# A tenth column unit by seven products, less filler in each attention cycle, and scalings that change engine

## The chip, the cores and the metric

The kernel runs on one core of one Trainium2 chip. The metric is the device time of one execution in microseconds (us), as the median of several runs. The core has five engines with queues of their own, and each queue runs in order: TensorE (PE, matrix products), VectorE (DVE), ScalarE (ACT), GpSimd (POOL) and SyncE (SP, which here only issues transfers). An engine that waits for something holds up everything that stands behind it in its queue.

## The reference

One encoder layer: RMS norm of x (2048 rows of 1024), one projection to q, k, v and a gate, neighbourhood attention with 16 heads of 64 over a grid of 32 rows by 64 columns, gating, an output projection with a residual, and a last RMS norm.

```python
h = rmsnorm(x, norm_0)
q, k, v, gate = split(h @ w_in_0, 4)                  # 2048 x 1024 each
for each grid row r, for each block of 16 query columns:
    s = q . k / 8 + bias    over 8 grid rows and 32 columns, -1e30 outside a window of 16 columns
    o = softmax(s) @ v
x = x + (o * silu(gate)) @ w_out_0
out = rmsnorm(x, norm_f)
```

All of it is in float32.

## The kernel before

Every float32 operand of a large product is split into a rounded high part and a low part, and a product is made of three TensorE instructions of 128x512 (high by high, high by low, low by high). Such an instruction is called a product here. The projection is cut into units: q, k and gate have four units each, named ("k", 3) and so on, and one unit gives two pairs of heads. Stage one works on the first 1024 rows, stage two on the last 1024. There `seven_products` computes a unit as a 2 by 2 block matrix in Strassen's way, with seven block products of 12 instructions, 84 in all, in place of the 96 of the plain way. Stage two does so with the units in `units_two`. What is left of the last 1024 rows (`halves`, computed by `group` in the plain way, 24 products for one output tile) is not computed there but kept as filler.

Then comes attention in 32 cycles, one for each pair of heads and quarter of the rows: eight cycles of row quarter 0, then sixteen that take quarters 1 and 2 in turn, then eight of quarter 3. Tiles of quarters 0 and 3 are smaller (11 and 12 key rows, against 15). Pass m of the loop at the end of the program issues, in this order:

- filler products through `feed`, `amount[m]` of them. After the first eight `normalise(2m-1)` is issued; it takes the reciprocal of the softmax sums and scales the four tiles of the second half of cycle m-1, two on GpSimd (L1168) and two on ScalarE (L1166)
- `turns(m-1)`: 44 transposes of the scaled tiles into six banks of PSUM, which ScalarE and VectorE copy to SBUF, three banks each (`pta`, L1183 and L1185)
- `scores(2m)` and `scores(2m+1)`: products of queries and keys (L1139); VectorE adds the bias and takes the maxima (L1148), ScalarE takes the exponential with the row sums (L1154). `normalise(2m)` is issued within and scales its four tiles on GpSimd
- `values(m-1)`: the products with v (L1213), and on VectorE the gating (`og`, L1217).

Below, "stretch m" is the time from the first transpose of pass m to that of pass m+1. In it the scores, the exponentials and the scalings of cycle m are made, and its filler is `amount[m+1]`, to within a few products. The filler's first part are the units left over; the rest are output rows: `outputs()` computes the tiles 0 to 5 (`PLAIN`) with `w_out` in the plain way, and VectorE adds the residual (`add_rows`, L1289), ScalarE squares (L1292). Weights are split for it on ScalarE and VectorE (`wh`/`wl`, `woh`/`wol`, L192 to L198), and so are the attention rows (`split_og`, `gh`/`gl`, L1259 and L1260). Of a finished tile `root` makes 1/sqrt with eight small VectorE instructions (L1316 to L1323), `scale` multiplies with two instructions of 128x512 (L1331), `send` stores.

Then `rows_by_seven` computes the ten last row tiles as five pairs by seven products, 35 blocks of 12 instructions, in the order of `seq`. A block (m, P) has its operand formed five blocks earlier (`form_rows`, L1465 and L1466). After P = 7 GpSimd issues a transfer that adds rows of x onto a tile kept in SBUF (`p`, L1480); after P = 4 VectorE adds that tile (L1289).

There is no scheduler: each engine's order is that in which the code issues. `store(key, lag, f)` delays f by `lag` filler products, and `due` runs what has come due.

```python
    dense, end_of_it = 16.5, 24
    amount = [dense] * 25
    for m in range(8, 24):
        amount[m] += 1.5 if m % 2 == 0 else -1.5
```

Of the kernel before, what the change touches and what calls it, by code (L numbers as in the profile page):

```python
# [76 lines left out]
def build(ctx, tc, x, xr, xt, wg, bias, w_out, n0, nf, out):  # L77
# [169 lines left out]
    def units(k, j):  # L247
        return [KINDS[k] + j + i for i in range(2 if k == "v" else 1)]

    units_two = [(k, j) for j in range(3) for k in "kqg"]  # L250
    halves = [(k, 3, 1, c) for g in ("k", "qg") for c in (2, 3) for k in g]
    attending = [False]
    last_use = {}
    for n, (k, j, ph, c) in enumerate(halves):
# [792 lines left out]
    def projections():  # L1047
        for n, (kind, j, ph, c) in enumerate(halves):
            state["half"] = n
            w = (KINDS[kind] + j, ph)  # L1050
            for a in range(2):
                if n == len(halves) - 5 and a == 0:
                    for k in range(RES_EARLY):
                        load_res(*turns_[k])
                if n == len(halves) - 1:
                    if a == 0:
                        load_og(0)
                        load_og(1)
                    else:
                        store(("og0",), 9, lambda: split_og(0))  # L1060
                consume(1)
                p = yield from group(w, a, c, n)
                state["event"] = clock[0]
                give(kind, 2 * j + a, c, p, True)
            state["done_halves"] = n + 1
# [91 lines left out]
    def normalise(i, both=False, between=None):  # L1157
        st = ST.pop(i)
        nc.vector.reciprocal(st[:, 8:12], st[:, 4:8])  # L1159
        for j, C in enumerate(pairs[i][2]):  # L1160
            if j and between:
                between()
            for s in range(2):
                o = 8 + 2 * j + s
                if both and j:
                    nc.scalar.activation(X[i, C][s], X[i, C][s], AF.Copy, scale=st[:, o:o + 1])  # L1166
                else:
                    nc.gpsimd.tensor_scalar(X[i, C][s], X[i, C][s], st[:, o:o + 1], 1.0, op0=OP.mult, op1=OP.mult)  # L1168

    spots = linear()  # L1170

# [170 lines left out]
        else:  # L1342
            roots.append((clock[0] + 8, n, root, scale, send))

    roots = []
    ended = [False]

    def run_roots(most=99):
        while roots and most and (roots[0][0] <= clock[0] or ended[0]):
            most -= 1  # L1350
            _, n, root, scale, send = roots.pop(0)
            root()
            store(("y", n), 18, scale)
            store(("y", n), 36, send)

    turns_ = [(0, 0), (1, 0), (2, 0), (0, 1), (1, 1), (2, 1)] + [(n, j) for n in range(3, PLAIN) for j in range(2)]
    place = {}
# [166 lines left out]
    def rows_by_seven():  # L1524
# [1 line left out]
            TF[f] = [(woh[4 * r + k, c], wol[4 * r + k, c]) for k in range(4)]  # L1526
        E, LEAD = 3, 5
        seq = [(m, P) for P in (1, 2) for m in range(E)]
        seq += [(0, 6), (1, 6), (0, 7), (0, 5), (1, 7), (0, 4), (1, 5), (0, 3), (1, 4), (2, 6), (1, 3), (3, 1), (2, 7), (2, 5), (2, 4), (2, 3)]
        seq += [(m, P) for m in range(E, len(PAIRS)) for P in order7 if (m, P) not in seq]  # L1530
        todo = {}

        def on(i, f, *a):
# [36 lines left out]
                        f(*a)  # L1570

    cycles = len(order)
    dense, end_of_it = 16.5, 24
    amount = [dense] * 25
    first = 16
    amount[0] -= first / 2
# [56 lines left out]
    for m in range(cycles + 1):  # L1633
        a = amount[m] - 8
        begin(m)
        feed(8)
        if m:
            due_here = []
            quiet[0] = True
            if a < 12 and m > 8 and m % 2:  # L1640
                normalise(2 * m - 1, True, lambda: due_here.append(split_rows() or consume(1, turn=True)))
            else:
                normalise(2 * m - 1, True)
            if a > 12:
                run_roots()
            elif not rows_due():
                run_roots(1)
            for k in range(3):
                if m == 1 and k == 2:
                    pass  # L1650
                elif a > 12 or not any(due_here) and (k < 1 or k < 2 and m > 8 and m % 2 == 0):
                    got = split_rows()
                    due_here.append(got)
                    if not got:
                        consume(1, turn=True)
                    elif a < 12 and m % 2 == 0 and len(items) - state["used"] == 8:
                        feed(a * 0.2)
                        consume(1, turn=True)
                feed(a * 0.2)
        else:  # L1660
            feed(a * 0.6)
        quiet[0] = False
        feed(a * 0.4, 8 if a > 12 else 4)
        if m:
            turns(m - 1)
        if m == cycles:
            all_loads()
            feed(6)
# [12 lines left out]
        if m:  # L1681
            values(m - 1)
        runs[0] += 1
        if m == 20:
            late_loads()
    ended[0] = quiet[0] = True
    store(("roots",), 8, run_roots)
    while next(outs, 0) != 0:
        due(1)
    rows_by_seven()  # L1690
# [32 lines left out]
```

## Time and profile before

| | |
|---|---|
| median of 3 runs | 1019.54 us (1019.34 to 1019.98) |
| the profiled execution | 1020.12 us, span 1018.4 us |
| TensorE clock granted | 0.999 |
| PE, busy share of the span | 99% |
| DVE, ACT, POOL | 73%, 53%, 16% |
| stage two by seven products | 400.86 to 572.23 us |
| attention, first transpose to last | 587.70 to 910.61 us |
| output rows by seven products | 914.95 to 1012.37 us |

Times in the rows are from the span's start. A row of the timeline gives the start, the time that an instruction or a run of like instructions took, the engine, the line, what it writes and reads, and in brackets how long the engine had been idle and what it waited for. Products are pipelined: one shows about 0.39 us but the next starts about 0.23 us later, so that PE can lose some tenths without looking idle; the distance of two starts is the surer measure.

### The profile page before, as it was taken

What the parts mean: (1) busy time and instruction counts of PE and PEld (TensorE: products, weight loads), DVE (VectorE), ACT (ScalarE), POOL (GpSimd) and SP (SyncE); (2) the same over time, 40 slices, a digit from 0 to 9 for tenths busy, and PEclk for the clock granted to TensorE, in tenths of its full rate; (3) what the DMA queues carried; (4) which work ended last, traced back from release to release, by engine and by line L of the source; (5) the groups of instructions that cost most, each with busy time, mean ns of one, the idle gap of its engine ahead of it and who ended that gap; (6) DMA issues with size and microseconds to landing.
All of it is one profiled execution on the core that took longest, in us unless ns stands there. A gap on an engine that the chain in (4) does not pass through costs nothing.

```text
span 1018.4 us, 19622 instructions
## 1 busy us (share of the span) xinstructions
PE 1007.5 (99%) x6952; PEld 803.5 (79%) x6952; DVE 744.4 (73%) x1648; ACT 537.2 (53%) x1305; POOL 165.8 (16%) x244
## 2 busy tenths in 40 slices
PE   9999999999999999999999999999999999999997
PEld 6888888888788888888888777777777777778876
DVE  5385878899798876766776566577777787677876
ACT  7655323434435442343433477678788867663433
POOL 0000132232132000000000023233232323221010
PEclk9999999999999999999999999999999999999999
DMA  9734676575537846657455787879888689799453
GB/s 307 251 104 115 188 214 220 173 228 185 166 104 217 255 126 185 201 175 225 168 197 191 224 261 242 261 224 289 268 260 267 205 257 298 208 358 362 134 156 104
DMA packets 142602, 218.23 MB, mean 214 GB/s; under 512 B 13032, under 2 KB 60392, under 8 KB 142504
## 3 DMA queue, kind: packets, MB, share of 16 engines
q1 hardware_dynamic: 140632, 213.96, 66.3%
q0 software_dynamic: 1440, 2.62, 1.6%
q8 instruction: 55, 0.90, 0.3%
q10 hardware_dynamic: 432, 0.40, 0.1%
q14 instruction: 43, 0.35, 0.1%
HBM read 151.92 MB, written 65.01 MB: 213 GB/s over the span
## 4 chain that ended last, share of the span: by engine, by line
PE 93%; DVE 3%; DMA 1%; ACT 1%; issue 1%; SPq 0%; ACTq 0%; DVEq 0%
PE pp L438 38%; PE py L1494 9%; PE pv L562 8%; PE o L1213 7%; PE pv L948 7%; PE s L1139 7%; PE ph L1194 4%; PE pp L384 2%; PE pp L386 2%; PE pp L382 2%; PE po L1412 2%; PE po L1414 2%; PE po L1416 2%; ACT x L1154 1%; DVE f L421 1%
## 5 line engine op out<-in xcount | busy, mean ns | idle before, releaser
L438 PE MATMUL pp<-h,f 128*128 128x512 f32 x672 | 217.3, 389 | 0.0
L1168 POOL TENSOR_SCALAR x<-x,st 128x360 f32<-128x360 f32 (+5 forms) x192 | 97.2, 523 | 482.8 <-DVE st L1159 480.9
L1154 ACT ACTIVATE x<-x,st 128x360 f32<-128x360 f32 (+5 forms) x256 | 134.1, 525 | 29.9 <-DVE st L1148 29.9
L438 PEld LDWEIGHTS pp<-h,f 128*128 128x128 f32 x672 | 126.1, 188 | 26.1
L438 PE MATMUL pp<-t,f 128*128 128x512 f32 x558 | 141.7, 389 | 0.1
L438 PE MATMUL pp<-l,f 128*128 128x512 f32 x336 | 130.7, 389 | 0.0
L438 PEld LDWEIGHTS pp<-t,f 128*128 128x128 f32 x558 | 104.6, 188 | 22.3 <-DVE u L451 0.6
L458 POOL TENSOR_TENSOR tmp<-tmp,rb 128x512 f32<-128x512 f32 x36 | 59.0, 1641 | 268.5 <-DVE tmp L456 233.4
L1148 DVE CUSTOM_DVE_ANT_0 x<-s,em 128x360 f32<-128x360 f32 (+5 forms) x256 | 101.5, 451 | 1.4 <-PE s L1139 1.4
L421 DVE TENSOR_TENSOR f<-raw,f 128x512 fp32r<-128x512 f32 x105 | 75.1, 715 | 29.3 <-ACT f L420 29.1
L1213 PEld LDWEIGHTS o<-pta,vt 120*64 120x64 f32 (+2 forms) x1024 | 68.7, 137 | 22.6 <-DVE st L1148 15.2
L1213 PE MATMUL o<-pta,vt 120*64 120x192 f32 (+5 forms) x1024 | 83.4, 316 | 0.3 <-issue 0.3
L420 ACT ACTIVATE f<-raw 128x512 fp32r<-128x512 f32 x105 | 63.6, 622 | 31.4 <-DMA raw<-in_wg_dram 13.3
L1139 PE MATMUL s<-kt,q 64*64 64x360 f32 (+5 forms) x1024 | 79.1, 421 | 0.6 <-DVE pta L1183 0.5
L1183 DVE COPY pta<-ph 120x512 f32<-120x512 f32 (+5 forms) x96 | 56.0, 637 | 30.9 <-PE ph L1194 30.5
L438 PEld LDWEIGHTS pp<-l,f 128*128 128x128 f32 x336 | 63.1, 188 | 13.2
L1185 ACT ACTIVATE pta<-ph 120x512 f32<-120x512 f32 (+5 forms) x96 | 46.7, 558 | 37.0 <-PE ph L1194 37.0
L1139 PEld LDWEIGHTS s<-kt,q 64*64 64x64 f32 x1024 | 39.6, 131 | 24.7 <-DVE pta L1183 6.1
L438 PE MATMUL pp<-sixths,f 128*128 128x512 f32 x198 | 54.6, 389 | 0.0
L420 ACT ACTIVATE f<-s 128x512 fp32r<-128x512 f32 x42 | 26.3, 625 | 52.9 <-DVE s L427 49.3
L1194 PEld LDWEIGHTS ph<-ident,x 64*120 64x120 f32 (+2 forms) x1408 | 42.6, 128 | 11.3 <-issue 10.6
L1494 PE MATMUL py<-woh,f 128*128 128x512 f32 x160 | 50.4, 390 | 0.0
(209 smaller groups left out, 1910.1 us busy)
## 6 DMA issues: line engine op xcount, KB each, us to landing
raw<-in_wg_dram SPq DMA_DIRECT2D x120, 256.0 KB, 4.9
row<-in_xr_dram SPq DMA_DIRECT2D x32, 256.0 KB, 5.3
vd<-v SPq DMA_DIRECT2D x32, 256.0 KB, 2.8
sgd<-sg SPq DMA_DIRECT2D x32, 256.0 KB, 3.6
q<-qd SPq DMA_DIRECT2D x32, 256.0 KB, 5.5
sgt<-sgd SPq DMA_DIRECT2D x32, 256.0 KB, 6.7
ogd<-og SPq DMA_DIRECT2D x32, 256.0 KB, 3.2
kt<-kd SPq DMA_DIRECT2D x16, 480.0 KB, 6.7
```

The costliest lines, as they stand in the source:

```text
L420: nc.scalar.activation(t[:, 0], src, AF.Copy)
L421: nc.vector.tensor_tensor(t[:, 1], src, t[:, 0].bitcast(F32), OP.subtract)
L438: nc.tensor.matmul(B[n, P], t[:, int(m == 2), c], x[k][int(m == 1)], start=P in (1, 6, 5) and k == 0 and m == 0, stop=k == 3 and m == 2, s ...
L562: nc.tensor.matmul(ps[t], a[:, o], b, start=k == 0 and m == 0, stop=k == NK - 1 and m == 2)
L948: nc.tensor.matmul(ps, a[:, o], b, start=P in (1, 6, 5) and k == 0 and m == 0, stop=k == 3 and m == 2, skip_group_check=True)
L1139: nc.tensor.matmul(pst[s][h * 64:h * 64 + 64], qt[a, g * 64:g * 64 + 64], kt[a, :r1 - r0, c0:c0 + 8 * WIDE[C]].rearrange("p r (s c) -> p s ...
L1148: nc.vector.tensor_tensor_reduce(X[i, C][s], pst[s], EM[p, ROW_TYPE[T]][C > 0][s], -1.0, 1e38, OP.add, OP.min, st[:, o:o + 1])
L1154: nc.scalar.activation(X[i, C][s], X[i, C][s], AF.Exp, bias=st[:, o:o + 1], scale=-1.0, accum_out=st[:, 4 + o:5 + o])
L1168: nc.gpsimd.tensor_scalar(X[i, C][s], X[i, C][s], st[:, o:o + 1], 1.0, op0=OP.mult, op1=OP.mult)
L1194: nc.tensor.transpose(ph[b, h][:k, o:o + 64], X[2 * m + late_, group[g]][s][q, at:at + k], ident[q, q])
L1213: nc.tensor.matmul(o[s * 64:s * 64 + 64, g0 * 64:g1 * 64], vt[:k, strip, s * 64:s * 64 + 64], t[:k, n * 64:(n + g1 - g0) * 64], start=stri ...
L1494: nc.tensor.matmul(B[m, P], t[:, a, c], b, start=P in (1, 6, 5) and k == 0 and i == 0, stop=k == 3 and i == 2, skip_group_check=True)
```

## The change

Five things are done.

1. The unit ("k", 3) moves from the filler to stage two. `units_two` has ten entries, `halves` four instead of six. 96 products leave the filler and 84 come to stage two, so that the program has 12 fewer.
2. `dense` goes from 16.5 to 13.6, and with the shorter sum what the last cycles get falls as well. Counted in the order of the code, the filler products of stretches 1 to 31 are, before: 18 15 16 17 16 17 18 15 18 15 21 12 21 15 17 15 18 15 18 15 18 15 16 17 16 17 19 14 16 18 20 (518), and after: 10 14 13 14 14 13 15 12 16 12 16 12 15 13 15 12 15 12 18 9 15 12 14 13 13 13 13 14 13 15 20 (425). The first loads of attention rows, of residual rows and of the last norm's weights (`late_loads`, after pass 8 instead of 20) move with it, and `split_og(0)` has a lag of 14.
3. In `normalise` the two scalings on ScalarE become VectorE `tensor_scalar` instructions, and the work that was issued between the two pairs of scalings (`between`: a split) is issued behind both.
4. `run_roots` issues the roots, and a new `run_scales` issues the scaling of the tiles whose root was made in an earlier pass, right behind the next `normalise`; before, `scale` came 18 products after the root, wherever that fell.
5. In `rows_by_seven` the last blocks of a pair, P = 3 and P = 4, come behind the first block of the next pair, in this order; before, each pair from the fourth on ran 1, 6, 2, 7, 5, 4, 3 (its first block in one case ahead of the pair before it).

```diff
-    units_two = [(k, j) for j in range(3) for k in "kqg"]
-    halves = [(k, 3, 1, c) for g in ("k", "qg") for c in (2, 3) for k in g]
+    units_two = [(k, j) for j in range(3) for k in "kqg"] + [("k", 3)]
+    halves = [(k, 3, 1, c) for c in (2, 3) for k in "qg"]
...
-                    if a == 0:
+                    if a == 1:
                         load_og(0)
                         load_og(1)
-                    else:
-                        store(("og0",), 9, lambda: split_og(0))
+                        store(("og0",), 14, lambda: split_og(0))
...
         for j, C in enumerate(pairs[i][2]):
-            if j and between:
-                between()
             for s in range(2):
                 o = 8 + 2 * j + s
                 if both and j:
-                    nc.scalar.activation(X[i, C][s], X[i, C][s], AF.Copy, scale=st[:, o:o + 1])
+                    nc.vector.tensor_scalar(X[i, C][s], X[i, C][s], st[:, o:o + 1], None, op0=OP.mult)
                 else:
                     nc.gpsimd.tensor_scalar(X[i, C][s], X[i, C][s], st[:, o:o + 1], 1.0, op0=OP.mult, op1=OP.mult)
+        if between:
+            between()
...
             root()
-            store(("y", n), 18, scale)
-            store(("y", n), 36, send)
+            rooted.append((n, scale, send))
+
+    def run_scales():
+        while rooted:
+            n, scale, send = rooted.pop(0)
+            scale()
+            store(("y", n), 18, send)
...
-        seq += [(0, 6), (1, 6), (0, 7), (0, 5), (1, 7), (0, 4), (1, 5), (0, 3), (1, 4), (2, 6), (1, 3), (3, 1), (2, 7), (2, 5), (2, 4), (2, 3)]
-        seq += [(m, P) for m in range(E, len(PAIRS)) for P in order7 if (m, P) not in seq]
+        seq += [(0, 6), (1, 6), (0, 7), (0, 5), (1, 7), (0, 4), (1, 5), (0, 3), (1, 4), (2, 6), (1, 3), (2, 7), (2, 5)]
+        for m in range(E, len(PAIRS)):
+            seq += [(m, 1), (m - 1, 3), (m - 1, 4), (m, 6), (m, 2), (m, 7), (m, 5)]
+        seq += [(len(PAIRS) - 1, 4), (len(PAIRS) - 1, 3)]
...
-    dense, end_of_it = 16.5, 24
+    dense, end_of_it = 13.6, 24
...
                 normalise(2 * m - 1, True)
+            run_scales()
             if a > 12:
                 run_roots()
...
-        if m == 20:
+        if m == 8:
             late_loads()
```

Line numbers of the changed program are a few lower or higher than those of the profile: L1182 is the copy of L1183, L1158 the reciprocal of L1159, L1330 the scaling of L1331, L1288 the addition of L1289.

The first place is stretch 10, on ScalarE, from the last exponential of the cycle to the copies of the next transposes. Before:

```order
L1154 ACTIVATE x_7047,st<-x_7047,st 128x360
L1154 ACTIVATE x_7048,st<-x_7048,st 128x360
L197 ACTIVATE woh<-raw 128x512
L1166 ACTIVATE x_7047<-x_7047,st 128x360
L1166 ACTIVATE x_7048<-x_7048,st 128x360
L197 ACTIVATE woh<-raw 128x512
L368 ACTIVATE q<-pp 128x512
```

The same place on ScalarE after the change:

```order
L1153 ACTIVATE x_7173,st<-x_7173,st 128x360
L1153 ACTIVATE x_7174,st<-x_7174,st 128x360
L1258 ACTIVATE gh<-ograw 128x512 x2
L1232 ACTIVATE acc_173<-acc_173 128x512
L1232 ACTIVATE acc_174<-acc_174 128x512
```

The two scalings are gone from ScalarE, and the split of the first attention rows (`gh`) stands where a weight's did. On VectorE the same stretch ran, from the gating to the copies of the next transposes, before:

```order
L1217 TENSOR_TENSOR og<-o,sgt 128x512
L1159 RECIPROCAL st<-st 128x4
L198 TENSOR_TENSOR wol<-raw,woh 128x512 x2
L1183 COPY pta<-ph_7124 120x8x64
L1183 COPY pta<-ph_7126 120x8x64
L1183 COPY pta<-ph_7128 120x6x64
```

And on VectorE after the change:

```order
L1216 TENSOR_TENSOR og<-o,sgt 128x512
L1259 TENSOR_TENSOR gl<-ograw,gh 128x512 x2
L1158 RECIPROCAL st<-st 128x4
L1163 TENSOR_SCALAR x_7173<-x_7173,st 128x360
L1163 TENSOR_SCALAR x_7174<-x_7174,st 128x360
L1182 COPY pta<-ph_7241 120x8x64
L1182 COPY pta<-ph_7243 120x8x64
L1182 COPY pta<-ph_7245 120x6x64
```

The low halves `gl` now stand ahead of the reciprocal, and the two scalings behind it.

The second place is stretch 20 on VectorE, likewise from the gating to the copies. Before:

```order
L1217 TENSOR_TENSOR og<-o,sgt 128x512
L198 TENSOR_TENSOR wol<-raw,woh 128x512
L1159 RECIPROCAL st<-st 128x4
L1289 TENSOR_TENSOR y<-po,xr 128x512
L1183 COPY pta<-ph_8905 120x8x64
L1183 COPY pta<-ph_8907 120x8x64
```

After the change, from the reciprocal on (two more small instructions on `st` follow, and then the copies):

```order
L1158 RECIPROCAL st<-st 128x4
L1163 TENSOR_SCALAR x_8909<-x_8909,st 128x360
L1163 TENSOR_SCALAR x_8910<-x_8910,st 128x360
L1330 SCALAR_TENSOR_TENSOR y<-y,st_7723,acc_173 128x512
L1330 SCALAR_TENSOR_TENSOR y<-y,st_7723,acc_174 128x512
L1315 TENSOR_SCALAR st_7937<-st_7937 128x1
L1316 TENSOR_SCALAR st_7937<-st_7937 128x1
L1317 TENSOR_SCALAR st_7937<-st_7937 128x1
L1318 SCALAR_TENSOR_TENSOR st_7937<-st_7937 128x1
L1319 SCALAR_TENSOR_TENSOR st_7937<-st_7937 128x1
L1320 SCALAR_TENSOR_TENSOR st_7937<-st_7937 128x1
```

A tile's scaling and another tile's root now stand between the reciprocal and the copies, in the stretch that has 9 filler products.

The third place is on VectorE in `rows_by_seven`, from the tile `u` that follows block (2, 7) to the addition of `p`, onto which GpSimd's transfer adds. Before:

```order
L1504 TENSOR_TENSOR u<-py,p_11081 128x512
L1511 TENSOR_TENSOR u<-u,xr 128x512
L1472 TENSOR_TENSOR raw<-raw 128x512
L1466 TENSOR_TENSOR f<-raw,f 128x512
L1289 TENSOR_TENSOR y<-py,u 128x512
L1466 TENSOR_TENSOR f<-raw,f 128x512
L1289 TENSOR_TENSOR y<-py,p_11081 128x512
```

After the change, without the first of these rows:

```order
L1515 TENSOR_TENSOR u<-u,xr 128x512
L1476 TENSOR_TENSOR s<-s,raw 128x512
L1470 TENSOR_TENSOR f<-s,f 128x512
L1330 SCALAR_TENSOR_TENSOR y<-y,st_11135,acc_173 128x512
L1330 SCALAR_TENSOR_TENSOR y<-y,st_11135,acc_174 128x512
L1288 TENSOR_TENSOR y<-py,u 128x512
L1476 TENSOR_TENSOR raw<-raw 128x512
L1470 TENSOR_TENSOR f<-raw,f 128x512 x2
L1288 TENSOR_TENSOR y<-py,u 128x512
L1476 TENSOR_TENSOR s<-raw,s 128x512
L1470 TENSOR_TENSOR f<-s,f 128x512
```

The addition of `p` is not among these rows, it comes four rows later: (2, 4) is now the fourth block after (2, 7), where it was the second.

More of the change, by code (lines that the diff above doesn't have):

```diff
@@ L1051, in projections @@
             for a in range(2):
-                if n == len(halves) - 5 and a == 0:
+                if n == 0 and a == 1:
                     for k in range(RES_EARLY):
@@ L1343, in finish @@
             roots.append((clock[0] + 8, n, root, scale, send))
-    roots = []
+    roots, rooted = [], []
     ended = [False]
```

2 lines of the change are left out of this document (1 added, 1 removed).

## The prediction

> **What bounds the kernel now.** First the page's table of engines and the chain of work that ended last, then the busy time by stage (stretch and its length, then PE, weight loads, VectorE, ScalarE, GpSimd, the clock, the share of the DMA engines, GB/s).
>
> ```profile
> PE 1007.5 (99%) x6952; PEld 803.5 (79%) x6952; DVE 744.4 (73%) x1648; ACT 537.2 (53%) x1305; POOL 165.8 (16%) x244
> ...
> PE 93%; DVE 3%; DMA 1%; ACT 1%; issue 1%; SPq 0%; ACTq 0%; DVEq 0%
> ```
>
> ```profile
> 400.86:572.23 171.37, 171.37 (x758) 141.90 (x757) 115.06 (x183) 62.80 (x112) 0.00 (x0) 1.00 0.62 198
> 584.00:914.90 330.90, 329.89 (x3960) 247.35 (x3958) 233.96 (x792) 246.92 (x734) 95.09 (x188) 1.00 0.83 261
> 914.90:1012.40 97.50, 95.76 (x422) 78.65 (x420) 75.67 (x147) 37.79 (x88) 8.81 (x10) 1.00 0.62 193
> ```
>
> TensorE is the bound in every stage, at full clock (1.00). In attention ScalarE is busy for 246.92 of 330.90 us and VectorE for 233.96, so neither is far from having to be in time for every cycle. What a product costs stands in the chain, in stage two, where PE runs without a gap:
>
> ```profile
> 400.86 171.36 PE pp L438 x756
> ```
>
> 171.36 / 756 = 0.2267 us. In attention I measure stretches, by the starts of their transposes on PE's timeline:
>
> ```profile
> 587.70 0.48 PE L1194 MATMUL ph<-ident,x 64*88 64x64 f32 x10
> ...
> 598.14 1.43 PE L1194 MATMUL ph<-ident,x 64*88 64x64 f32 x44
> ...
> 701.16 1.51 PE L1194 MATMUL ph<-ident,x 64*120 64x64 f32 x44
> ...
> 710.52 1.51 PE L1194 MATMUL ph<-ident,x 64*120 64x64 f32 x44
> ...
> 763.22 1.51 PE L1194 MATMUL ph<-ident,x 64*120 64x64 f32 x44
> ...
> 773.85 1.51 PE L1194 MATMUL ph<-ident,x 64*120 64x64 f32 x44
> ...
> 847.11 1.10 PE L1194 MATMUL ph<-ident,x 64*96 64x64 f32 x32
> ...
> 858.71 0.98 PE L1194 MATMUL ph<-ident,x 64*96 64x64 f32 x28
> ...
> 869.44 0.76 PE L1194 MATMUL ph<-ident,x 64*96 64x64 f32 x20
> ...
> 910.61 0.59 PE L1194 MATMUL ph<-ident,x 64*96 64x64 f32 x14
> ```
>
> Stretch 12 (701.16 to 710.52) is 9.36 us with 12 products, so 6.64 without them; stretch 27 (858.71 to 869.44) is 10.73 with 19, so 6.42. Stretch 1 (587.70 to 598.14, 18) gives 6.36. By these, the 31 stretches from 587.70 to 910.61 should take 518 x 0.2267 + 7 x 6.36 + 17 x 6.64 + 7 x 6.42 = 319.8 us and took 322.9: 3.1 us are lost in attention.
>
> **How long a stretch must be.** Stretch 12 has as few products as most of the changed ones. Its rows on VectorE, GpSimd (with one of an earlier stretch) and ScalarE:
>
> ```profile
> 708.83 0.18 DVE L1159 RECIPROCAL st<-st 128x4 f32<-128x4 f32 x1 [0.44 <-ACT x L1154]
> 709.35 0.93 DVE L198 TENSOR_TENSOR wol<-raw,woh 128x512 fp32r<-128x512 f32 x1 [0.34 <-ACT woh L197]
> 711.51 1.75 DVE L1183 COPY pta<-ph 120x512 f32<-120x512 f32 x3
> ...
> 697.78 1.11 POOL L1168 TENSOR_SCALAR x<-x,st 128x360 f32<-128x360 f32 x2 [0.33 <-DVE st L1159]
> 709.18 1.53 POOL L1168 TENSOR_SCALAR x<-x,st 128x360 f32<-128x360 f32 x2 [0.33 <-DVE st L1159]
> ...
> 708.71 0.61 ACT L197 ACTIVATE woh<-raw 128x512 fp32r<-128x512 f32 x1
> 711.24 1.47 ACT L1185 ACTIVATE pta<-ph 120x512 f32<-120x512 f32 x3 [0.42 <-PE ph L1194]
> ```
>
> Counted from its first transpose: ScalarE is through with the exponentials at 7.55, the reciprocal runs from 7.67 to 7.85, GpSimd's scalings end at 9.55 (9.13 had they taken the 1.11 us of the other row). The next transposes begin at 9.36, but the tiles scaled last belong to their second half, from 10.08 (half of the 1.44 us that they take behind one another). So 0.53 us were left and nothing was lost. The copies started 0.99 us after the transposes on VectorE and 0.72 on ScalarE. What it costs when they start late:
>
> ```profile
> 763.23 0.68 DVE L1289 TENSOR_TENSOR y<-po,xr 128x512 f32<-128x512 f32 x1
> ...
> 763.94 0.63 ACT L1292 ACTIVATE xr<-y 128x512 f32<-128x512 f32 x1 [1.44 <-DVE y L1289]
> 764.58 1.44 ACT L1185 ACTIVATE pta<-ph 120x512 f32<-120x512 f32 x3
> ...
> 848.04 1.41 DVE L1331 SCALAR_TENSOR_TENSOR y<-y,st,acc 128x512 f32<-128x512 f32 x2
> 849.37 1.74 DVE L1183 COPY pta<-ph 96x512 f32<-96x512 f32 x3
> ```
>
> In stretch 18 a square ahead of ScalarE's copies made them 0.64 us late (764.58 - 763.22 - 0.72), and the stretch (10.63 with 15 products) lost 0.59. In stretch 26 the scaling of a tile made VectorE's 1.27 late, and it lost 1.33 (11.60 with 17). The scores need the banks that the copies free; lateness is lost about one to one.
>
> **The change, part by part.**
>
> *The tenth unit.* 96 products out, 84 in: 12 x 0.2267 = 2.72 us less. Stage two has room: VectorE was busy 115.06 us of 171.37 there.
>
> *The scalings.* ScalarE loses two instructions a cycle; VectorE gets two. The nearest row is the last tile's scaling, 128x512:
>
> ```profile
> L1328 DVE TENSOR_SCALAR yw<-yw,st x2: 486/488/489, 1011.8 to 1014.3; 128x512 f32<-128x512 f32 x2
> ```
>
> 0.34 (by size) to 0.49 us each; I take 0.75 for two, since small ones have a fixed part. They end at 8.6, before GpSimd's. How much they hold GpSimd up the trace doesn't show; beside L198 its two took 1.53 instead of 1.11. The bounds are 0 and 0.75, and with the whole 0.75 they end at 9.88, 0.2 before 10.08. I take no loss in a stretch of 12. The Trainium skill (SBUF — State Buffer, "Who interferes with whom") has VectorE's fast `tensor_scalar` and GpSimd exclude each other for whole instructions, and that speaks against the move: by it the full 0.75 would count, and work with two operands in SBUF behind it would add to it. The slowed GpSimd row agrees in kind.
>
> *The shorter stretches.* The products that leave them are counted above; what remains is which stretch becomes late. I go through the orders of VectorE and ScalarE with these rows and three more: the split of attention rows, the root (the first of its eight small instructions, and what came next) and a reciprocal of quarter 3:
>
> ```profile
> 855.42 1.14 ACT L1259 ACTIVATE gh<-ograw 128x512 fp32r<-128x512 f32 x2
> ...
> 856.07 1.47 DVE L1260 TENSOR_TENSOR gl<-ograw,gh 128x512 fp32r<-128x512 f32 x2 [0.34 <-ACT gh L1259]
> ...
> 823.89 0.18 DVE L1316 TENSOR_SCALAR st<-st 128x1 f32<-128x1 f32 x1
> 825.81 0.69 DVE L1289 TENSOR_TENSOR y<-po,xr 128x512 f32<-128x512 f32 x1
> ...
> 876.58 0.18 DVE L1159 RECIPROCAL st<-st 128x4 f32<-128x4 f32 x1
> ```
>
> - Stretch 20 (9 products, 8.68 long): scalings to 8.6, a tile's scaling 1.41 to 10.0, a root 1.92 (823.89 to 825.81) to 11.9. VectorE's copies would start at 9.67: 2.2 lost.
> - Stretch 10 (12): `gl` stands ahead of the reciprocal and ends 2.12 after `gh` starts, at 9.67 instead of the reciprocal's 7.67. 2.0 late, less the 0.95 from 9.13 to 10.08: 1.1 lost.
> - Stretch 25 (13, quarter 3): an addition and a split stand ahead of the reciprocal, and the split is of the tile that PE takes next, after five products, at 6.42 + 1.13 = 7.55. `gh` starts when the exponentials are done, about 7.0 (stretch 28 has its reciprocal at 876.58 - 869.44 = 7.14); half of `gl` is done 1.4 later (856.07 + 0.73 - 855.42), at 8.4 to 8.7: 1.0 lost.
> - Stretch 23 (14, 9.81 long): scalings 8.6, a tile's scaling 10.0, then `y` and the square ahead of ScalarE's copies, 1.35 as in stretch 18 (763.23 to 764.58): 11.35 instead of 10.53, 0.8 lost.
> - Stretches 11, 14 and 22 come to a few tenths late; 0.3 together. The others end early.
>
> Sum 5.4, where 3.1 is lost now. What makes those 3.1 goes, as far as I can place it: scalings of tiles no longer fall just ahead of the copies in 26, the square of 18 moves, the weights that stretch 20 waited for are split by stretch 16. So attention loses 2.3 us. Ends: 0.4 (only the small ones come, -2.7) and 10.3 (the rival below, +7.2).
>
> *The roots and loads* cost nothing of their own: as many instructions, on queues that have gaps; their place is counted above.
>
> *The order of the pairs.* The one idle time of PE among the 420 products at the end:
>
> ```profile
> 982.13 1.17 PE L1494 MATMUL py<-t,f 128*128 128x512 f32 x4 [1.67 <-ACT f L1465]
> ...
> 980.80 0.20 ACT L1311 ACTIVATE st<-st 128x1 f32<-128x1 f32 x1 [1.32 <-DVE st L1310]
> ...
> 975.43 0.69 DVE L1289 TENSOR_TENSOR y<-py,p 128x512 f32<-128x512 f32 x1 [3.38 <-PE py L1494]
> ...
> 969.21 0.86 POOL L1480 DMA_DIRECT2D p<-in_x_dram  x1 [7.27 <-DVE u L1504]
> ...
> DMA to landing us min/median/max: 3.9/4.6/6.1
> ```
>
> PE waited 1.67 us for an operand that stood behind a root on ScalarE, which stood behind VectorE's addition of `p`. That one is put down to PE, but its block, the 21st, was done about 972; what came at 975.3 is GpSimd's transfer, 969.21 + 6.1. After the change (2, 4) is the fourth block behind (2, 7), 10.9 us instead of 5.4, and the transfer has landed. I take all 1.67 off. Above 0 the bound is another late operand: (4, 1) is formed in the step in which its rows are asked for, and PE takes it five blocks (13.6 us) later, more than the 5 or so that such a load takes.
>
> **Sum.** -2.72 + 2.3 - 1.67 = -2.1. The profiled execution took 1020.12 (1.7 of it outside the span), which gives 1018.0; it lay 0.58 above the median, so I forecast 1019.54 - 2.1 = 1017.4 us.
>
> **The rivals.**
>
> *The late stretches don't come.* For: the lateness is built from single rows, and ScalarE has 64 scalings less to do in attention. Against: VectorE's order in stretch 20 leaves little choice. Then attention loses 0.4 instead of 3.1: 1019.54 - 2.72 - 2.7 - 1.67 = 1012.4; with half of it, 1015.
>
> *GpSimd becomes the bound of the short stretches (slower).* Held up by both VectorE scalings and by the whole of a 0.93 us instruction behind them, its scalings end at 9.13 + 0.75 + 0.93 = 10.81, 0.73 after the second half of the transposes wants them. Stretches 8, 12, 14, 16, 18, 20 and 22 are short and have such work: 7 x 0.7 = 4.9, so 1022.3. It decides once more than 0.2 us comes on top of the 0.75. For: the 1.53; against: there one instruction of 0.93 cost only 0.42.
>
> *The end isn't saved*, since another in-order wait takes its place: 1017.4 + 1.67 = 1019.1, no change.
>
> **How the numbers follow.** Forecast 0.50, its own range 1015.8 to 1019.2; late stretches not there 0.25; GpSimd 0.16; end not saved 0.09. A measurement here can tell about 0.2%, 2.04 us: the border to faster is 1017.5, at the forecast itself, so half of the forecast's chance is faster and half no change. Faster 0.25 + 0.25 = 0.50, no change 0.25 + 0.09 = 0.34, slower 0.16. The range is 1013.0 to 1022.0; about 1 in 10 is left out on either side.
>
> **What would show it.** Right: stage two 19 us longer; stretches of 12 products 9.4 us long; stretches 10, 20, 23 and 25 one to two us longer than 6.64 (6.42) plus their products; no gap among the last 420 products, and the addition of `p` without an idle time of 3 us. Wrong: every short stretch of quarters 1 and 2 longer than its products allow, with GpSimd's L1165 near 2 us (the GpSimd rival), or stretch 20 at 8.7 us (the late stretches not there).

## The result, and the profile after

The changed kernel took 1026.36 us (median of 5 runs, 1025.19 to 1027.18), the one before 1019.54 beside it. The ratio is 1.0064, with a 95% interval of 1.0053 to 1.0076: slower by 6.5 us (6.8 by the two medians), where 2.1 us faster was forecast. All ratios here compare executions that ran beside each other, and leave out the one of 2031.64 us among the nine of the kernel with all three places moved. The profiled execution took 1025.54 us, 1023.8 of it in the span, against 1020.12 and 1018.4 before.

The page's table of engines and the same three stages of the changed kernel (columns as before), and its longest piece of stage two in the chain of work that ended last:

```profile
PE 1009.9 (99%) x6940; PEld 804.7 (79%) x6940; DVE 782.8 (76%) x1724; ACT 507.8 (50%) x1242; POOL 174.1 (17%) x244
```

```profile
400.86:591.00 190.14, 190.14 (x841) 157.44 (x840) 127.11 (x202) 70.13 (x124) 0.00 (x0) 1.00 0.60 190
591.00:920.00 329.00, 323.55 (x3925) 240.00 (x3925) 267.72 (x872) 216.09 (x677) 105.46 (x192) 1.00 0.84 263
920.00:1018.00 98.00, 96.85 (x436) 79.60 (x432) 77.11 (x148) 39.06 (x90) 8.83 (x10) 1.00 0.64 195
```

```profile
400.73 190.40 PE pp L438 x840
```

Stage two is 19.04 us longer (190.40 for 171.36), still without a gap and at 0.2267 us a product. VectorE went up in attention and ScalarE down, and both are still far from full. PE's busy share says nothing of the loss; its transposes do:

```profile
605.93 1.43 PE L1193 MATMUL ph<-ident,x 64*88 64x64 f32 x44
615.25 1.43 PE L1193 MATMUL ph<-ident,x 64*88 64x64 f32 x44
625.44 1.04 PE L1193 MATMUL ph<-ident,x 64*88 64x64 f32 x23
...
636.85 1.43 PE L1193 MATMUL ph<-ident,x 64*88 64x64 f32 x44
...
704.42 0.81 PE L1193 MATMUL ph<-ident,x 64*120 64x64 f32 x20
...
715.77 1.73 PE L1193 MATMUL ph<-ident,x 64*120 64x64 f32 x44
726.00 1.51 PE L1193 MATMUL ph<-ident,x 64*120 64x64 f32 x44
...
805.07 1.58 PE L1193 MATMUL ph<-ident,x 64*120 64x64 f32 x44
817.49 1.51 PE L1193 MATMUL ph<-ident,x 64*120 64x64 f32 x44
...
847.23 1.43 PE L1193 MATMUL ph<-ident,x 64*96 64x64 f32 x44
858.06 1.51 PE L1193 MATMUL ph<-ident,x 64*96 64x64 f32 x44
...
916.83 1.43 PE L1193 MATMUL ph<-ident,x 64*96 64x64 f32 x44
```

By the prediction's rule (length less 6.36, 6.64 or 6.42, less 0.2267 a product), stretch 3 (625.44 to 636.85, 13 products) lost 2.10 us, stretch 11 (704.42 to 715.77, 16) 1.08, stretch 12 (12) 0.87, stretch 21 (805.07 to 817.49, 15) 2.38, stretch 25 (847.23 to 858.06, 13) 1.46. From the first transposes to the last, attention took 310.90 us (605.93 to 916.83) where it took 322.91: 12.01 less. 93 products less are 21.08, so the losses rose from 3.14 us to 12.21, by 9.07. The rest of the span's 5.4: up to the first transposes +18.23 (19.04 in stage two; with three products fewer between it and the transposes), and 0.82 less from the last transposes to the end (106.97 for 107.79).

All 12.21 us, by stretch: 1 0.69, 2 0.66, 3 2.10, 5 0.41, 11 1.08, 12 0.87, 15 0.35, 17 0.68, 19 0.15, 21 2.38, 24 0.83, 25 1.46, 26 0.19; the others together 0.36. The rule is good to about 0.2 us: stretch 24 comes out at -0.17 in the first and the fourth experiment below.

### The profile page after: what moved, and what is told of

Read it like the earlier page. It is cut to its first block, busy times and chain, and to the rows that moved or that the text cites. A ratio compares the mean times of both kernels' runs of the same rounds, so it can differ in the third digit from the quotient of the medians.

```text
span 1023.8 us, 19602 instructions
## 1 busy us (share of the span) xinstructions
PE 1009.9 (99%) x6940; PEld 804.7 (79%) x6940; DVE 782.8 (76%) x1724; ACT 507.8 (50%) x1242; POOL 174.1 (17%) x244
## 3 DMA queue, kind: packets, MB, share of 16 engines
q0 software_dynamic: 1440, 2.62, 1.7%
## 4 chain that ended last, share of the span: by engine, by line
PE 90%; DVE 5%; ACT 3%; issue 1%; DMA 1%; POOL 0%; SPq 0%; POOLq 0%; DVEq 0%; ACTq 0%
PE pp L438 39%; PE pv L562 9%; PE py L1498 7%; PE pv L948 7%; PE s L1138 7%; PE o L1212 7%; PE ph L1193 4%; PE po L1418 2%; PE po L1416 2%; ACT x L1153 2%; PE po L1420 2%; PE pp L384 1%; PE pp L386 1%; PE pp L382 1%; DVE y L1330 1%
## 5 line engine op out<-in xcount | busy, mean ns | idle before, releaser
L438 PE MATMUL pp<-h,f 128*128 128x512 f32 x704 | 227.8, 389 | 0.0
L1165 POOL TENSOR_SCALAR x<-x,st 128x360 f32<-128x360 f32 (+5 forms) x192 | 105.5, 567 | 480.3 <-DVE st L1158 478.0
L438 PEld LDWEIGHTS pp<-h,f 128*128 128x128 f32 x704 | 132.1, 188 | 27.5
L438 PE MATMUL pp<-t,f 128*128 128x512 f32 x584 | 148.4, 389 | 0.1
L438 PE MATMUL pp<-l,f 128*128 128x512 f32 x352 | 136.9, 389 | 0.0
L438 PEld LDWEIGHTS pp<-t,f 128*128 128x128 f32 x584 | 109.5, 188 | 23.3 <-DVE u L451 0.6
L421 DVE TENSOR_TENSOR f<-raw,f 128x512 fp32r<-128x512 f32 x110 | 78.6, 714 | 28.8 <-ACT f L420 28.5
L420 ACT ACTIVATE f<-raw 128x512 fp32r<-128x512 f32 x110 | 66.6, 622 | 33.2 <-DMA raw<-in_wg_dram 13.1
L438 PEld LDWEIGHTS pp<-l,f 128*128 128x128 f32 x352 | 66.1, 188 | 13.6
L1182 DVE COPY pta<-ph 120x512 f32<-120x512 f32 (+5 forms) x96 | 55.9, 636 | 19.9 <-PE ph L1193 19.6
L456 DVE TENSOR_TENSOR tmp<-pp,u 128x512 f32<-128x512 f32 x44 | 30.3, 689 | 29.5 <-PE pp L438 25.2
```

The lines of the kernel that those rows point to most:

```text
L420: nc.scalar.activation(t[:, 0], src, AF.Copy)
L421: nc.vector.tensor_tensor(t[:, 1], src, t[:, 0].bitcast(F32), OP.subtract)
L438: nc.tensor.matmul(B[n, P], t[:, int(m == 2), c], x[k][int(m == 1)], start=P in (1, 6, 5) and k == 0 and m == 0, stop=k == 3 and m == 2, s ...
```

## The experiments

Each is read by what attention lost, by the rule above, and by its time. Spans of single executions are less sure: PE began stage two between 399.96 us (the sixth run) and 402.35 (the last), by when no edit has had an effect; the traces differ from the first 10 us on, where PE waits for the first loads.

### The scalings back on ScalarE

```diff
-    nc.vector.tensor_scalar(X[i, C][s], X[i, C][s], st[:, o:o + 1], None, op0=OP.mult)
+    nc.scalar.activation(X[i, C][s], X[i, C][s], AF.Copy, scale=st[:, o:o + 1])
```

> The changed kernel with the two scalings of each cycle back on ScalarE, all else changed. Theory FILLER (the stretches are too short for the in-order queues, whichever engine scales): 1024 to 1027 us, within 1.5 us of the changed kernel, and about 10 us still lost in attention. Theory SCALINGS (VectorE's two scalings hold up GpSimd's, 1.85 us instead of 1.11, and fill VectorE): 1018 to 1021 us, and less than 6 us lost in attention.

1023.93 us, ratio 1.0050 (1.0035 to 1.0065); attention lost 10.88 us. The time lies just under what FILLER gives, the loss fits it. The scalings on VectorE are not the cause of most of it: without them 7.7 us more than before the change is still lost. But they have a part in it: stretches 1 and 2 lost nothing here, and 3 lost 1.15 in place of 2.10, with the same filler.

### The order of the pairs alone

The kernel before, with the changed `seq` and nothing else.

> The kernel before with nothing but the new order of the last blocks of the output pairs. If the 1.67 us of idle TensorE at the end go, as forecast: 1017.5 to 1018.3 us (-1.2 to -2.0). If, as in the changed kernel's trace, another wait of about 1 us takes its place: 1018.6 to 1019.3. Attention as before, 3.1 us lost.

1019.52 us, ratio 1.0001 (0.9991 to 1.0010). Attention lost 3.15 us as before, and the end became 0.82 us shorter in the profile (106.97 for 107.79). PE's 1.67 us are gone, and a new wait of 0.90 stands at 970.09. The new order moves the end by less than the runs can tell.

### Nine units, with the scalings and roots as changed

```diff
-    units_two = [(k, j) for j in range(3) for k in "kqg"] + [("k", 3)]
+    units_two = [(k, j) for j in range(3) for k in "kqg"]
...
-    dense, end_of_it = 13.6, 24
+    dense, end_of_it = 16.5, 24
```

(with the six `halves`, their loads, the lag of 9 and `late_loads` at 20 as before the change)

> The changed kernel with nine units in stage two, 16.5 products of filler and the loads as before: scalings on VectorE, roots and scales issued anew and the order of the pairs stay. FILLER: 1017 to 1020 us, since the longer stretches hide VectorE's work. SCALINGS: 1022 to 1026 us.

1019.88 us, ratio 1.0004 (0.9995 to 1.0014). Attention lost 5.08 us, 3.53 of it in stretch 24. The time is FILLER's.

### Ten units alone

The kernel before, with the first two parts of the change: ten units, 13.6 a run, the loads that go with them.

> The kernel before with ten units, 13.6 products and the loads that go with it; scalings on ScalarE, roots, scales and the order of pairs as before. FILLER: 1023 to 1028 us, 9 us or more lost in attention. SCALINGS: 1016 to 1019 us, 3 to 5 us lost.

1022.91 us, ratio 1.0035 (1.0022 to 1.0047). Attention lost 9.45 us, for the most part in the same stretches: 3 1.20, 5 0.48, 11 0.88, 12 1.34, 21 1.53, 25 1.46, 26 0.98 and smaller ones, and nothing in 1, 2 and 24. So of the three parts the smaller filler is what costs most: 6.3 us more are lost for the 2.7 that twelve products save. (The time is again just under FILLER's range.) What stood open was whether a stretch of 12 to 14 products is too short as such, or whether single instructions in it stand in bad places.

### Three places, one at a time

*The split of attention rows.* In stretch 10 it stood ahead of the reciprocal; a later lag puts it behind.

```diff
-                        store(("og0",), 14, lambda: split_og(0))
+                        store(("og0",), 17, lambda: split_og(0))
```

> The changed kernel with one number changed: the first attention rows are split 17 products after their load instead of 14, which puts gh and gl of stretch 10 behind the reciprocal and the scalings. Theory PLACES (each loss comes from a few instructions that stand ahead of a reciprocal or of the copies in a short stretch, and goes with them): the 1.08 us lost in stretch 11 go, the rest stays, 12.2 lost becomes 11.1, 1025 to 1026 us. Theory SHORTNESS (the stretches are too short whatever stands where, and what is saved in one is lost in the next): lost stays 12 within 0.5.

1025.48 us, ratio 1.0049 (1.0034 to 1.0064). Stretch 11's loss went from 1.08 to under 0.05 (counting a product that moved from it to stretch 10), the others stayed within 0.1: 11.21 us.

*The units of x.* In the changed kernel the x of row quarter 3 is normalised (L516, L520) inside stretches 1 and 2. This is VectorE of the changed kernel at the end of stretch 2, from behind the gating to the copies, and ScalarE (`sg` is the gate's own activation, for a unit of filler):

```profile
624.59 0.69 DVE L363 SCALAR_TENSOR_TENSOR sg<-sg,pp 128x512 f32<-128x512 f32 x1 [1.74 <-ACT sg L362]
625.20 0.17 DVE L1158 RECIPROCAL st<-st 128x4 f32<-128x4 f32 x1
625.40 0.86 DVE L1163 TENSOR_SCALAR x<-x,st 128x264 f32<-128x264 f32 x2
626.18 0.96 DVE L516 SCALAR_TENSOR_TENSOR raw<-raw,g,rb 128x512 f32<-128x512 f32 x1
...
628.45 1.74 DVE L1182 COPY pta<-ph 88x512 f32<-88x512 f32 x3
...
627.18 0.63 ACT L520 ACTIVATE h<-raw 128x512 fp32r<-128x512 f32 x1 [2.62 <-DVE raw L516]
627.72 1.44 ACT L1184 ACTIVATE pta<-ph 88x512 f32<-88x512 f32 x3
```

ScalarE waits 2.62 us for VectorE's product, squeezes its own step in and copies 2.28 us after the transposes began (627.72 less 625.44) instead of 0.68. VectorE then waits for ScalarE's step, and its copies start 3.01 us after the transposes instead of 0.94 (the values of quarter 0): 2.07 late, and stretch 3 lost 2.10.

```diff
-        xi = [("x", b, c) for b in range(4)] if c == 3 and c not in seen else []
+        xi = [("x", b, 3) for b in range(4)] if n == 0 else []
...
-        items += xi + wi
+        items += wi + xi
```

> The changed kernel with the four row tiles of x taken before the gate's weights, so that stretches 0 to 2 hold weight splits (ScalarE first, one VectorE instruction) where they held normalisations (VectorE, ScalarE, VectorE). PLACES: the 3.45 us lost in stretches 1 to 3 become 1.2 or less, 1023.5 to 1025 us. SHORTNESS: 3 or more are still lost there.

1024.16 us, ratio 1.0044 (1.0027 to 1.0060). Attention lost 9.89 us: stretches 1 to 3 fell from 3.45 to 1.08, the others stayed. For the 1.08 that is left in stretch 3 the trace points to `sg` (L363), which still stands ahead of the reciprocal: GpSimd's scalings end 1.69 us after the first transpose, and the first and the last of the 44 transposes start 2.34 us apart instead of 1.21. No run moved `sg`. And it takes both, the x units and the scalings on VectorE, to lose what came back: with the scalings on ScalarE and x where it was, stretches 1 to 3 lost about 1.2 us (the first and the fourth experiment).

*The root beside a tile's scaling.* VectorE of the changed kernel at the end of stretch 20, and the root's last instruction before the copies (its transposes began at 805.07):

```profile
804.27 1.04 DVE L1163 TENSOR_SCALAR x<-x,st 128x360 f32<-128x360 f32 x2
805.23 1.70 DVE L1330 SCALAR_TENSOR_TENSOR y<-y,st,acc 128x512 f32<-128x512 f32 x2
806.86 0.20 DVE L1315 TENSOR_SCALAR st<-st 128x1 f32<-128x1 f32 x1
...
808.37 0.16 DVE L1322 SCALAR_TENSOR_TENSOR st<-st 128x1 f32<-128x1 f32 x1
808.45 1.75 DVE L1182 COPY pta<-ph 120x512 f32<-120x512 f32 x3
```

The copies start 3.38 us after the transposes, 2.39 later than 0.99; the next stretch lost 2.38.

```diff
             scale()
+            scaled[0] = runs[0]
...
-            if a > 12:
+            if scaled[0] == runs[0]:
+                pass
+            elif a > 12:
                 run_roots()
```

> The changed kernel with no root issued in a pass that has issued a tile's scaling, so that stretch 20 (9 products) holds the scaling alone. PLACES: of the 2.38 us lost in stretch 21 at most 0.5 stay, 1024 to 1025 us. SHORTNESS: the root only moves the loss to stretch 22, and the sum stays at 12 within 0.5.

1023.79 us, ratio 1.0035 (1.0022 to 1.0049). Attention lost 10.64 us. Without the root the copies there start 1.79 us after the transposes, 0.80 late:

```profile
804.83 1.57 PE L1193 MATMUL ph<-ident,x 64*120 64x64 f32 x44
...
815.70 1.51 PE L1193 MATMUL ph<-ident,x 64*120 64x64 f32 x44
```

```profile
804.99 1.71 DVE L1330 SCALAR_TENSOR_TENSOR y<-y,st,acc 128x512 f32<-128x512 f32 x2
806.62 1.74 DVE L1182 COPY pta<-ph 120x512 f32<-120x512 f32 x3
```

and the stretch takes 10.87 us, a loss of 0.83. So 1.55 of the 2.38 went and more stayed than the 0.5 that was expected: the tile's scaling alone still makes the copies late.

### The three places together, with the scalings on ScalarE and on VectorE

First with the first experiment's edit added, which had seemed a gain:

> The three edits together, and the scalings back on ScalarE. PLACES: lost 5 to 6 us in attention (sg ahead of the reciprocal in 4 and 11, squares in 14 to 19, the late split in 25 and 26 stay), 1018.5 to 1020.5 us. SHORTNESS: 1022 us or more.

A miss: 1025.51 us, ratio 1.0051 (1.0036 to 1.0066); attention lost 10.92 us. Stretches 1 and 2 were clean and 21 lost 0.74, but 9, 12 to 15, 19 and 26 lost 5.3 together. With the scalings on ScalarE the three edits brought next to nothing (10.88 without them): stretches 1 and 2 had lost nothing there to begin with. Then the same three edits with the scalings left on VectorE:

> The changed kernel with all three places moved (the items of x last, the split of attention rows behind the reciprocal, the root in a cycle without a tile's scaling), the scalings of the pair's second half still on VectorE. Places add up: each of the three savings was seen alone (2.4 us in stretches 1 to 3, 1.0 in stretch 11, 1.6 in stretch 21), so attention loses 12.2 - 5.0 = 7.2 us, stretches 12 and 25 as before (0.9 and 1.5), and the time is about 1021.4 us. Total of items (the short stretches have too little room, whatever stands where): what one stretch no longer loses shows in another, the loss stays near 10 us as with the scalings on ScalarE, and the time stays at 1024 or above.

1021.77 us, ratio 1.0022 (1.0011 to 1.0033); attention lost 7.23 us, where the sum of the three single savings had given 7.2. The time came 0.4 us above the forecast. The two kernels differ in one line, and the place at which stretch 12's loss is made shows one way in which the 3.7 us between them come about. ScalarE with the scalings on it, then VectorE of that run:

```profile
714.15 1.08 ACT L1163 ACTIVATE x<-x,st 128x360 f32<-128x360 f32 x2 [0.90 <-DVE st L1158]
715.14 1.14 ACT L1258 ACTIVATE gh<-ograw 128x512 fp32r<-128x512 f32 x2
...
715.79 1.29 DVE L1259 TENSOR_TENSOR gl<-ograw,gh 128x512 fp32r<-128x512 f32 x2 [1.73 <-ACT gh L1258]
717.00 0.68 DVE L198 TENSOR_TENSOR wol<-raw,woh 128x512 fp32r<-128x512 f32 x1
717.60 1.74 DVE L1182 COPY pta<-ph 120x512 f32<-120x512 f32 x3
```

VectorE with the scalings on it:

```profile
712.42 1.56 DVE L1259 TENSOR_TENSOR gl<-ograw,gh 128x512 fp32r<-128x512 f32 x2
713.90 0.68 DVE L198 TENSOR_TENSOR wol<-raw,woh 128x512 fp32r<-128x512 f32 x1
714.51 1.74 DVE L1182 COPY pta<-ph 120x512 f32<-120x512 f32 x3
```

On ScalarE the scalings need VectorE's reciprocal, the split `gh` stands behind them, VectorE waits 1.73 us for `gh`, and its copies start 2.42 us after the transposes (715.18): 1.43 late, and 1.43 lost. On VectorE they do not stand in `gh`'s way, and the copies start 1.97 after the transposes (712.54): 0.98 late, 0.97 lost. That is 0.46 of the 3.7; the other stretches were not taken apart. So moving the scalings was right for this schedule, by 3.7 us of loss once the places are mended.

### Nine units with the root apart

The third experiment's kernel, with the `scaled` edit.

> Nine units as before the change, filler of 16.5 a run, the scalings on VectorE, the scalings of tiles kept back, the new order of pairs, and the root in a cycle without a tile's scaling. With the root beside it stretch 24 lost 3.53 us of the 5.08. Places: most of that goes (the tile's scaling alone is 1.41 us, of which up to 0.5 is lost), attention loses 1.5 to 2.5 us, the span is 3 us shorter than with the root beside it and the time about 1017 us. The other theory (something else than the root makes stretch 24 late): stretch 24 still loses over 2 us, and the time is 1019 to 1020.

1019.25 us, ratio 0.9998 (0.9989 to 1.0007). Stretch 24 fell from 3.53 to 0.43, so it was the root. But stretch 27 now lost 1.32 (3.32 in all), and the end became 1.9 us longer (108.9 for 107.0): PE waited in a new place.

```profile
938.57 6.61 PE L1500 MATMUL py<-t,f 128*128 128x512 f32 x28 [1.66 <-ACT f L1471]
```

### The tile's scaling ten products earlier

The kernel before with the new order of pairs, and this:

```diff
-            store(("y", n), 18, scale)
-            store(("y", n), 36, send)
+            store(("y", n), 8, scale)
+            store(("y", n), 26, send)
```

> The kernel before with the new order of the pairs, and a tile's scaling due 8 instead of 18 products behind its root (its store 26 instead of 36). The two scalings leave stretch 25, where they stood last ahead of the copies, and stand ahead of the reciprocal in stretch 23, and behind a root in stretches 27 and 30. Places: the 1.33 us that stretch 26 lost goes, and 0.3 to 0.6 us is lost behind 23 in its place; with 0.8 at the end, 1017.5 to 1018.5 us. If it isn't the place: 1019.5, as with the new order alone.

1020.16 us, ratio 1.0007 (0.9997 to 1.0016). The 1.31 that stretch 26 lost with the new order alone went to under 0.05, as expected; but stretch 24 lost 1.29 (0.20 with the new order alone), and attention 3.24. The end came to 108.51 us, with a wait of 1.26 us at 937.88, in the place of the 1.66 of the run before. The gain that was forecast did not come.

### Nine units, the root apart and not beside a split

```diff
-            if scaled[0] == runs[0]:
+            if scaled[0] == runs[0] or any(due_here):
```

> Nine units with the root apart once more, and now no root in a cycle that has split attention rows either. Two things changed at the end with the root apart: stretch 27 lost 1.32 us (two halves of a split, a root and an addition stood ahead of the copies), and PE waited 1.66 us at 938.57 for attention rows, whose loads stood on SP's queue directly behind the stores of a tile (900.08, then 902.00, instead of 903.02 without them, with all transfers 2 us further ahead). Now these stores leave SP's queue about 16 issues earlier, where they stand with the root beside the scaling, and the root of stretch 26 moves to 27. Places: stretch 27 loses 0.2 at most, PE doesn't wait at 938, attention loses about 2 us, the last transposes lie 107 us from the end, the span is 1016 to 1016.7, and the time some 2 us below the kernel before, about 1017.5. If the wait at 938 comes from attention that ends earlier (the loads' rate is the bound, not what stands ahead of them): PE still waits 1 to 1.7 us there, and the time is 1019.

1018.80 us, ratio 0.9992 (0.9983 to 1.0001). Attention lost 2.02 us, the least of all runs, stretch 27 nothing, and PE did not wait at 938. SP's queue of the run with the wait, the stores of a tile and the loads of attention rows:

```profile
900.08 1.39 SPq L1335 DMA_DIRECT2D out_dram<-y  x2
902.00 4.96 SPq L1466 DMA_DIRECT2D raw<-ogd  x6
...
923.73 0.90 SPq L1466 DMA_DIRECT2D raw<-ogd  x2
```

And without it:

```profile
889.06 0.91 SPq L1335 DMA_DIRECT2D out_dram<-y  x2
899.95 4.24 SPq L1466 DMA_DIRECT2D raw<-ogd  x6
...
922.69 0.90 SPq L1466 DMA_DIRECT2D raw<-ogd  x2
```

With the stores some 14 issues earlier, the loads are issued earlier (902.00 to 899.95, and 923.73 to 922.69), and the rows are there in time. How late the last of these loads lands goes with the wait: counted from the last transposes, it landed at 16.8 us in the second and the third run and 17.4 here, without a wait; at 18.5 in the eleventh (1.26 us of wait) and 18.9 in the tenth (1.66). That the stores make it late is not shown. In the eleventh run PE waited too, and no stores of a tile stood directly ahead of the six loads:

```profile
880.81 1.18 SPq L1335 DMA_DIRECT2D out_dram<-y  x2
...
900.98 4.00 SPq L1460 DMA_DIRECT2D raw<-ogd  x6
...
922.64 0.90 SPq L1460 DMA_DIRECT2D raw<-ogd  x2
```

So the other reading of the expectation, that the rate of the transfers is the bound, is open. The places came as expected, the 1017.5 us did not. By the medians it is 7.6 us faster than the changed kernel; compared with the one before, its 0.8 us cannot be told from nothing.

## Why the prediction was wrong, point by point

**The tenth unit: right.** 12 products of 0.2267 us less, stage two longer by 19.04 without a gap.

**A stretch of 12 is long enough: right, as far as it was tried.** What comes late at the end of a stretch is lost in the next one, so it is the stretches behind the short ones that tell. Behind 8, 12, 18 and 22 (12 products each) 0.01, 0.01, 0.15 and 0.07 us were lost. Behind 10 (12) and 20 (9) 1.08 and 2.38 were lost, of which moving the split took back all and moving the root 1.55. Behind 16 (12) 0.68 were lost, with an addition ahead of the reciprocal; that one was not tried.

**The failed step is the walk through the shorter stretches**, where it said "Stretches 11, 14 and 22 come to a few tenths late; 0.3 together. The others end early." The four places that it worked out came about in the way it says, and nearly in size: 1.1 forecast for stretch 10 and 1.08 seen, 2.2 for 20 and 2.38, 0.8 for 23 and 0.83, 1.0 for 25 and 1.46: 5.75 for 5.1. (The size for stretch 20 is in part luck: the two scalings took 1.05 us, not 0.75, the tile's scaling 1.70, not 1.41, and the root 1.6, not 1.92. The loss shows in the length of the stretch after the late copies, 11, 21 and 24; stretch 20 itself took 8.69 us. So one of the prediction's own signs, "stretch 20 at 8.7 us", read the wrong side of the transposes.) What was given 0.3 lost 6.46:
- 3.86 in stretches 1, 2, 3 and 5, which the walk does not name. By it quarter 0 ends early, and before the change it was clean, with 18 15 16 17 products; with 10 14 13 14 the x units and `sg` fall among the last instructions ahead of the copies. Moving the x units alone took back 2.37 of it. Of this the scalings on VectorE are the other half of the cause, as the first experiment shows.
- 0.87 in stretch 12, from a split, a weight's low half and `sg` in stretch 11, which the walk had at a few tenths.
- 1.73 in smaller pieces: 0.68 in 17, 0.35 in 15 (behind stretch 14, one of the three at a few tenths), and less in 19, 26, 28 and others.

The two rows that the walk rests on, copies at +0.99 and lateness lost one to one, held in the four places shown, where VectorE's copies were the late ones (2.39 late and 2.38 lost, 0.80 and 0.83, 1.43 and 1.43, 0.98 and 0.97). The method was right; its result for the stretches that it did not name was not.

**The scalings: their sizes were wrong.** Two on VectorE took 1.05 us, not 0.75. They held GpSimd up by up to the bound of 0.75, here in stretch 11 of the changed kernel, against 1.11 us:

```profile
714.59 1.05 DVE L1163 TENSOR_SCALAR x<-x,st 128x360 f32<-128x360 f32 x2
715.56 1.56 DVE L1259 TENSOR_TENSOR gl<-ograw,gh 128x512 fp32r<-128x512 f32 x2
...
714.74 1.84 POOL L1165 TENSOR_SCALAR x<-x,st 128x360 f32<-128x360 f32 x2 [1.55 <-DVE st L1158]
```

Where no such instruction stands behind the scalings, the two on GpSimd took less:

```profile
774.11 1.34 POOL L1165 TENSOR_SCALAR x<-x,st 128x360 f32<-128x360 f32 x2 [0.32 <-DVE st L1158]
```

So the scalings cost GpSimd 0.2, and the two low halves behind them 0.5 more. The Trainium skill (SBUF — State Buffer, "Who interferes with whom") has the two engines exclude each other there, which agrees in kind; that the full time of the scalings would count, as the prediction took from it, the 0.2 does not bear out. The GpSimd rival did not decide: PE's wait for GpSimd's scalings ahead of the transposes grew to

```profile
PEld ph L1193 <- POOL x L1165: 5.7, 15, 0.6
```

from 0.7 us in 2 waits, and it was 5.1 us with the scalings on ScalarE too: it comes with the shorter stretches, not with VectorE. Not all of it is lost. In stretches 3, 5, 11 and 17 the transposes do stall (their first and last start 1.7 to 2.4 us apart instead of 1.2 to 1.3), and in each `sg`, the split or an addition stood ahead of the reciprocal that GpSimd waits for.

**The roots "cost nothing of their own": by place they did.** The prediction had counted their places, and 2.2 us in stretch 20 held one of them. A root behind a tile's scaling cost 1.6 us in stretch 21, and 3.1 in stretch 24 with nine units, where the third experiment's kernel differed from the tenth's in that alone.

**The order of the pairs: half right.** VectorE's wait for `p` and PE's 1.67 us are gone:

```profile
982.43 0.69 DVE L1288 TENSOR_TENSOR y<-py,p 128x512 f32<-128x512 f32 x1
```

but PE waits for a bank instead, some 12 us earlier, counted from the last transposes, as it does with the new order alone (VectorE, then PE):

```profile
974.54 1.41 DVE L1330 SCALAR_TENSOR_TENSOR y<-y,st,acc 128x512 f32<-128x512 f32 x2
975.87 0.68 DVE L1288 TENSOR_TENSOR y<-py,u 128x512 f32<-128x512 f32 x1
...
976.69 0.47 PE L1498 MATMUL py<-woh,f 128*128 128x512 f32 x1 [0.90 <-DVE y L1288]
```

VectorE's addition, which frees it, stands behind the scaling of a tile. The end gained 0.82 us, not 1.67. This is the third rival's mechanism, at half its size.

Put together for the profiled executions: -2.72 + 9.07 - 0.82 = +5.5 us; the sum had -2.72 + 2.3 - 1.67. The runs say 6.5 (5.4 to 7.8).

What stays open: no run went after the 7.2 us that the ninth run still lost. Its trace has VectorE's copies late in 12, 15 and 21 (2.1 us lost), stalled transposes in 3, 5 and 17 (2.2), PE waiting for the halves of a split in 25 (1.45) and ScalarE's copies late in 24 (0.83). Its time lies 2.2 us above the kernel before, where its losses, products and end give 0.5. The two profiled executions differ by 0.68 (1020.80 and 1020.12), as that sum has it; but the first was the fastest of its kernel, and the second lay 0.58 above its median. So the sum explains the traces, and the rest of the 2.2 is not explained.

## What to carry to other kernels

When filler is taken from a loop whose copies stand on in-order queues, write down for every pass, the first ones too, what stands between the last operand of the cycle and the copies, and compare its end with the time that the copies are due: each lateness of VectorE's copies that was followed up was lost one to one, and of the three losses that were tried, moving one item took back one whole and more than half of each of the others. The place of an instruction counted for more than the engine it runs on: the same scalings looked harmful in one order and saved 3.7 us in the other. And where a step is moved, look at what it pulls along, down to the stores and loads: with the root apart and nine units, attention lost 1.8 us less and the end took 1.9 more.

## What the runs showed of the hardware that was not expected

A tile's scaling on VectorE (L1330, two instructions of 128x512) took 1.41 us where GpSimd was idle, and 1.70 to 1.71 directly behind the new scalings, where GpSimd's ran into the first of the two (1.04 us for it and 0.74 for the second, in stretch 20 of the changed kernel). GpSimd's own two took 1.34 there, no more than without a two-operand instruction behind them. In the first experiment it went the other way: there the tile's scaling started first, at 806.01 us, and its two instructions took 0.72 and 0.75 while GpSimd's two, which started 0.25 us later, took 2.02. So where the two overlap, now one engine is held up and now the other.
